# New durations in the table by which a kernel orders its own work

## The chip, the cores and the metric

The kernel runs on one core of one Trainium2 chip. The metric is the device time of one launch in microseconds. The core has a matrix engine (TensorE, PE in the rows; its weight loads are PEld), a vector engine (VectorE, DVE), a scalar engine (ScalarE, ACT), GpSimd (POOL) and the DMA queues (started here from SyncE, SP). Each engine works through its own instructions strictly in the order in which the program emitted them; semaphores make one engine wait for another.

## The reference

Six layers in float32 on a sequence of 1024 (from the fourth on 1040, with 16 meta tokens ahead), width 1024:

```python
# first_block
f1 = swiglu(rms_norm(x, g), w_gate, w_up, w_down);  x = x + 0.5 * rms_norm(f1, g2)      # ffn1, 2816 wide
m  = token_mixer(rms_norm(x, g3), ...);             x = x + rms_norm(m, g4)             # mixer
f2 = swiglu(rms_norm(x, g5), ...);                  x = x + 0.5 * rms_norm(f2, g6)      # ffn2
# token_mixer: 8 causal softmax heads with a decay (fox) and 4 pairs of softmax heads whose difference is taken (diff)
# second_block, on concat(meta, x)
h = rglru_ssd_layer(h)         # even layer: a gated linear recurrence and a chunked state-space scan
# odd layer: 16 heads of stick-breaking attention
z        = q @ k.T * 64**-0.5
log_keep = where(before, log_sigmoid(-z), 0);  csum = cumsum(log_keep)
weights  = where(before, exp(log_sigmoid(z) + csum[-1] - csum), 0)
o        = (weights @ v) * silu(g);            h = h + o @ w_out
return rmsnorm(h)[16:]
```

## The kernel before

All products are made as three matmuls on split operands (high part times high part, low times high, high times low; `mm3`, L334 to 338), accumulated in PSUM. Whatever comes out of PSUM is therefore taken twice: ACT casts the high part, DVE subtracts it to leave the low part.

**What sets the order.** The program doesn't list its instructions in a fixed order. Each piece of work is a generator, a thread, that yields pairs of an engine (P for PE, A for ACT, V for DVE, G for POOL, D for a DMA) and an estimated duration, and then emits the instruction. `Sched` (L109 to 197) keeps for each engine the time at which it will be free, and for each thread the time at which its input is there; `run` always takes the thread whose request can start first, ties by the thread's priority and then its age:

```python
            start = max(ready, self.free[eng])
            switch = self.switch(th[3])
            key = (start + self.TABLE * switch, th[0], th[1])
```

`ready` is the end of the thread's last step, plus HOP = 0.45 us when that was on another engine; TABLE = 0.8 us is the price of changing ACT's function table. The estimates come from four functions at L93 to 106: `pe(n, passes)`, `act(n)`, `dve(n, speed)` and `pool_tt(n)`, n being the columns of the operand. A duration in them thus changes no instruction; it changes which of two instructions is emitted first. Priorities: the evacuation of transposed weights and the value products 0, attention scores and weights 1, weight streams 2, evacuations of projections 3, projections themselves 5.

**The odd stage**, on which the prediction dwells. 16 heads in 8 pairs. For each block of 128 queries: PE makes scores `psc` (L1540, 1541, with a mask matmul L1543); `weights` (L2263 to 2281) puts two sigmoids on ACT (`kt`, `pt`), a running product over the row on DVE (`tensor_tensor_scan`, L2275) and the product of both on DVE (L2279). Then `pv_group` (L1558 on): PE transposes the weights into PSUM (`ptr`, L1607); `pt_evac` lets ACT cast the high part (`th`, L224) and DVE the low part (`tl`, L1552); PE multiplies `th` and `tl` with the values into `po` (L1587). Two `th`, three `tl`, three `ptr` banks are in rotation. Between these, PE's filler is the projection of later head pairs (`pq`, `pk`, `pv`, `pg`: L336 to 338 and L1525 to 1527), which waits for nothing but its PSUM banks (two, freed by an ACT and a DVE step each). The mixer does the same with softmax in place of `weights`. **The even stage** has 1024- and 1040-column operations on DVE (L2553, 2781, 3002), the recurrence (L3015) and the gate product `sz` (L2601), which frees the bank of the projection `pe`. The feed-forward stages are streams of large matmuls.

Of the kernel before, what the change touches and what calls it, by code (L numbers as in the profile page):

```python
# [22 lines left out]
L = M + S  # L23
# [71 lines left out]


def act(n):
    return 0.07 + 0.92e-3 * n


def dve(n, speed=1):
    return 0.08 + 1.045e-3 * n / speed


def pool_tt(n):
    return 0.2 + 2.1e-3 * n


class Sched:  # L109
# [91 lines left out]
class Ctx:  # L201
# [53 lines left out]
    def act_t(self, *args, **kw):  # L255

        self.pin = self.after_pin(self.nc.scalar.activation(*args, **kw))
# [171 lines left out]
class Stream:  # L429
# [38 lines left out]
    def split(self, raw, hi, lo, n, ev, eng, free=True):  # L468
        nc = self.c.nc
        yield ("A", act(n))  # L470
        nc.scalar.copy(hi, raw)
        t = yield (eng, pool_tt(n) if eng == "G" else dve(n))
        (nc.gpsimd if eng == "G" else nc.vector).tensor_sub(lo, raw, hi.bitcast(F32))  # L473
        if free:
            self.r_raw.release(t)
        if ev is not None:
            ev.set(t)
# [898 lines left out]
class Attention:  # L1376
# [30 lines left out]
    def event(self, *key):  # L1407
        return self.ev.setdefault(key, Ev())
# [365 lines left out]
def mixer_stage(c, A, rows0, prm, w_in, forget_b, lams, subln, rope, w_out, gpost, res, rows):  # L1774
# [3 lines left out]
    with ExitStack() as ctx:  # L1778
# [11 lines left out]
        def gate(lf, h):  # L1790
            yield T.r_ps["mm"]
            ps = c.ps("mm", "pg")
            t = yield from gemm(c, ps[:8], W.w["gate"], A, HALVES[h], T.ev_A[h])
            sch.spawn(gate_evac(lf, HALVES[h], ps), 1, t)
            return t

        def gate_evac(lf, tok, ps):
            yield r_rx
            x = pp.tile([8, 512], F32, tag="rx", name="gx", bufs=2)
            e = pp.tile([8, 512], F32, tag="ry", name="ge", bufs=2)  # L1800
            t = yield ("V", dve(512))
            nc.vector.tensor_scalar(x, ps[:8], fb, None, op0=ALU.add)
            T.r_ps["mm"].release(t)
            yield ("A", act(512))
            nc.scalar.activation(e, x, AF.Abs)
            yield ("A", act(512))
            nc.scalar.activation(e, e, AF.Exp, scale=-1.0)
            yield ("A", act(512))
            nc.scalar.activation(e, e, AF.Ln, bias=1.0)
            yield ("V", dve(512, 2))  # L1810
            nc.vector.tensor_scalar(x, x, 0.0, None, op0=ALU.min)
            t = yield ("V", dve(512))
            nc.vector.tensor_sub(lf[:, tok], x, e)
            r_rx.release(t)
            if tok is HALVES[1]:
                cum = pm.tile([8, S], F32, tag="bc", name="cum", bufs=2)
                yield ("V", dve(1024))
                nc.vector.tensor_tensor_scan(cum, c.one[:8].to_broadcast([8, S]), lf, 0.0, op0=ALU.mult, op1=ALU.add)
                t = yield ("D", 0.3)
                nc.sync.dma_start(cD, cum)  # L1820
                r_bc.release(t + 1.0)
                r_bc.release(t + 1.0)
                T.event("cum").set(t + 2.0)
# [132 lines left out]
        def softmax(segs, m, pt, cb, ev, r):  # L1956
            ns = len(segs)
            small = lambda nm: c.small.tile([P, 2], F32, tag=nm, name=nm, bufs=8)
            mx, sm = small("mx"), small("sm")
            for s, ps in enumerate(segs):  # L1960
                yield ("V", dve(m))
                if cb is not None:
                    nc.vector.tensor_tensor_reduce(ps[:, :m], ps[:, :m], cb[:, s * m:s * m + m], 1.0, 3e38,
                                                   ALU.add, ALU.min, accum_out=mx[:, s:s + 1])
                else:
                    nc.vector.tensor_reduce(mx[:, s:s + 1], ps[:, :m], axis=AX.X, op=ALU.min)
            if ns == 2:
                yield ("V", 0.2)
                nc.vector.tensor_tensor(mx[:, 0:1], mx[:, 0:1], mx[:, 1:2], op=ALU.min)
            for s, ps in enumerate(segs):  # L1970
                t = yield ("A", act(m))
                nc.scalar.activation(pt[:, s * m:s * m + m], ps[:, :m], AF.Exp, bias=mx[:, 0:1], scale=-1.0,
                                     accum_out=sm[:, s:s + 1])
                T.r_ps["sc"].release(t)
            yield ("V", 0.2 * ns)
            if ns == 2:
                nc.vector.tensor_add(sm[:, 0:1], sm[:, 0:1], sm[:, 1:2])
            nc.vector.reciprocal(sm[:, 0:1], sm[:, 0:1])
            n = ns * m
            if cb is not None:  # L1980
                yield ("V", dve(n, 2))
                nc.vector.tensor_scalar(pt[:, :n], pt[:, :n], sm[:, 0:1], None, op0=ALU.mult)
            r.append(sm[:, 0:1])
            ev.set(sch.time)
# [205 lines left out]
def odd_stage(c, A, rows0, prm, w_in, w_out, res, final, out):  # L2190
# [3 lines left out]
    with ExitStack() as ctx:  # L2194
# [68 lines left out]
        def weights(ps, w, kt, k0, m, before, scanned, done):  # L2263

            yield ("A", act(m))
            nc.scalar.activation(kt[:, k0:k0 + m], ps[:, :m], AF.Sigmoid, scale=-1.0)
            t = yield ("A", act(m))
            nc.scalar.activation(w[:, k0:k0 + m], ps[:, :m], AF.Sigmoid)
            T.r_ps["sc"].release(t)
            if before is not None:  # L2270
                yield before

            t = yield ("V", dve(m))
            rev = kt[:, k0:k0 + m][:, ::-1]
            nc.vector.tensor_tensor_scan(rev, rev, c.one.to_broadcast([P, m]), kt[:, k0 + m:k0 + m + 1],  # L2275
                                         op0=ALU.mult, op1=ALU.mult)
            scanned.set(t)
            t = yield ("V", dve(m))
            nc.vector.tensor_mul(w[:, k0:k0 + m], w[:, k0:k0 + m], kt[:, k0 + 1:k0 + m + 1])  # L2279
            if k0 == 0:  # L2280
                r_kt.release(t)
                done.set(t)
# [187 lines left out]
LH = L // 2  # L2470
# [28 lines left out]
def even_stage(c, A, rows0, prm, w_in, lru_wa, lru_wx, dt_bias, a_log, ssd_d, w_out, meta, res, rows, later):  # L2499
# [151 lines left out]
    def dt_tile(nm):  # L2651
        dts[nm] = yield from SL.get(nm)
        return dts[nm][1][:NH, :L]
# [14 lines left out]
    def dt_rest():  # L2668
        for i in range(4):
            yield event("dt", i)  # L2670
        l = yield from dt_tile("l")
        dt, cut, ac = (dts[nm][1][:NH, :L] for nm in ("dt", "cut", "ac"))
        yield ("A", act(L))
        nc.scalar.activation(l, dt, AF.Abs)
        yield ("A", act(L), SET_LNEXP)
        act_t(l, l, AF.Exp, scale=-1.0)
        yield ("A", act(L), SET_LNEXP)
        act_t(l, l, AF.Ln, bias=1.0)
        yield ("A", 0.2, SET_LNEXP)
        act_t(na, na, AF.Exp)  # L2680
        yield ("V", dve(L))
        nc.vector.scalar_tensor_tensor(dt, dt, 0.0, l, op0=ALU.max, op1=ALU.add)
        yield ("V", 0.2)
        nc.vector.tensor_scalar(na, na, -1.0, None, op0=ALU.mult)

        nc.gpsimd.memset(cut, 1.0)
        for t0, _ in CHUNKS:
            nc.gpsimd.memset(cut[:, t0:t0 + 1], 0.0)
        yield ("V", dve(L, 2))
        nc.vector.tensor_scalar(l, dt, na, None, op0=ALU.mult)  # L2690
        yield ("V", dve(L))
        nc.vector.tensor_tensor_scan(ac, cut, l, 0.0, op0=ALU.mult, op1=ALU.add)
        t = yield ("D", 0.5)
        nc.sync.dma_start(aD, ac)
        event("aD").set(t + 2.0)

        yield ss
        psd = c.ps("ss", "psd")[:, :288].rearrange("p (c a h) -> p c a h", c=9, a=2)
        yield ("P", 1.0)
        for i, (t0, T) in enumerate(CHUNKS):  # L2700
            nc.tensor.transpose(psd[:T, i, 0], dt[:, t0:t0 + T], c.ident[:NH, :NH])
            nc.tensor.transpose(psd[:T, i, 1], ac[:, t0:t0 + T], c.ident[:NH, :NH])
        t = yield ("V", 0.6)
        nc.vector.tensor_copy(dT[:M, 0], psd[:M, 0])
        nc.vector.tensor_copy(dT[:, 1:], psd[:, 1:])
        ss.release(t)
        for i, _ in dts.values():
            SL.release(t + 1.0, i)
        event("dT").set(t)
# [270 lines left out]
    def lru_rest(b, h, r, ig, t_, v):  # L2980
# [28 lines left out]
        t = yield ("V", dve(L))  # L3009
        nc.vector.tensor_mul(vf, vf, gf)  # L3010
        SL.release(t, ii)
        for j in range(2):
            u = 2 * b + j
            t = yield ("V", dve(LH, 0.5))
            nc.vector.tensor_tensor_scan(t_[:, j], r[:, j], v[:, j], 0.0 if h == 0 else carry[:, u:u + 1], op0=ALU.mult,  # L3015
                                         op1=ALU.add)
            if h == 0:
                nc.gpsimd.tensor_copy(carry[:, u:u + 1], t_[:, j, LH - 1:LH])
# [290 lines left out]
```

## Time and profile before

| | |
|---|---|
| time before, median of 3 runs | 3578.08 us (3573.04 to 3578.96) |
| profiled execution, own time | 3577.13 us |
| its span | 3575.4 us, 51885 instructions |
| PE | 3430.7 us busy, 96% |
| DVE | 2749.9 us busy, 77% |
| ACT | 1700.6 us busy, 48% |
| POOL | 326.1 us busy, 9% |
| granted TensorE clock, mean of the span | 0.987 |

The stages follow each other on PE; those named below are the mixer (730 to 1250 us of the span), the even stage (2010 to 2600) and the odd stage (2835 to 3460). Busy times count durations; as two neighbouring instructions of an engine can overlap, starts are what tells how fast it takes the next one.

### The profile page before, as it was taken

What the parts mean: (1) busy time and instruction counts of PE and PEld (TensorE: products, weight loads), DVE (VectorE), ACT (ScalarE), POOL (GpSimd) and SP (SyncE); (2) the same over time, 40 slices, a digit from 0 to 9 for tenths busy, and PEclk for the clock granted to TensorE, in tenths of its full rate; (3) what the DMA queues carried; (4) which work ended last, traced back from release to release, by engine and by line L of the source; (5) the groups of instructions that cost most, each with busy time, mean ns of one, the idle gap of its engine ahead of it and who ended that gap; (6) DMA issues with size and microseconds to landing.
All of it is one profiled execution on the core that took longest, in us unless ns stands there. A gap on an engine that the chain in (4) does not pass through costs nothing.

```text
span 3575.4 us, 51885 instructions
## 1 busy us (share of the span) xinstructions
PE 3430.7 (96%) x19675; PEld 2925.6 (82%) x19675; DVE 2749.9 (77%) x5050; ACT 1700.6 (48%) x3451; POOL 326.1 (9%) x355
## 2 busy tenths in 40 slices
PE   8999999899999999999999899998999999999998
PEld 6788888678888877888888899988878888888877
DVE  8876699988888769666799779578633688878784
ACT  5323245556666643232345447447422465656561
POOL 0111144000000001111351000000000000000000
PEclk9999999999999999999999999999999999999999
DMA  5542372311211551323552334244473110111133
GB/s 183 178 132 89 113 284 83 128 58 44 73 41 36 179 168 60 123 89 109 195 197 72 108 64 86 61 87 90 139 244 95 57 36 28 33 31 31 33 134 107
DMA packets 305842, 366.07 MB, mean 102 GB/s; under 512 B 18644, under 2 KB 221568, under 8 KB 305592
## 3 DMA queue, kind: packets, MB, share of 16 engines
q1 hardware_dynamic: 299800, 341.71, 30.7%
q10 hardware_dynamic: 5792, 21.04, 1.6%
q8 instruction: 155, 2.54, 0.3%
q14 instruction: 95, 0.78, 0.1%
HBM read 267.58 MB, written 95.13 MB: 101 GB/s over the span
## 4 chain that ended last, share of the span: by engine, by line
PE 73%; DVE 17%; ACT 4%; issue 3%; DMA 2%; SPq 0%; POOL 0%; DVEq 0%; ACTq 0%; POOLq 0%
PE pst L337 7%; PE pst L336 7%; PE pst L338 7%; PE po L1587 3%; PE pe L336 3%; PE pe L338 3%; PE pe L337 3%; DVE kt L2275 3%; PE pdn L337 2%; PE pdn L338 2%; PE pdn L336 2%; PE ptr L1607 2%; PE pwo L3100 2%; PE pwo L3101 2%; PE pwo L3102 2%
## 5 line engine op out<-in xcount | busy, mean ns | idle before, releaser
L336 PE MATMUL pe<-Ah,wh 128*128 128x260 f32 (+1 forms) x1184 | 340.6, 288 | 21.9 <-DVE sz L2601 8.2
L338 PE MATMUL pe<-Ah,wl 128*128 128x260 f32 (+1 forms) x1184 | 337.1, 285 | 0.0
L337 PE MATMUL pe<-Al,wh 128*128 128x260 f32 (+1 forms) x1184 | 336.4, 285 | 0.0
L224 ACT CAST wh<-w 128x512 fp32r<-128x512 f32 x280 | 162.1, 619 | 252.7 <-PE pst L337 160.2
L942 DVE TENSOR_TENSOR sg<-sg,pst 128x512 f32<-128x512 f32 x280 | 187.1, 684 | 104.8 <-PE pst L338 104.4
L1006 POOL TENSOR_TENSOR h<-h 128x512 f32<-128x512 f32 x88 | 136.2, 1547 | 1332.9 <-DVE h L988 1327.7
L337 PE MATMUL pst<-Al,wh 128*128 128x512 f32 x640 | 253.7, 396 | 0.0
L336 PE MATMUL pst<-Ah,wh 128*128 128x512 f32 x640 | 252.2, 394 | 0.0
L338 PE MATMUL pst<-Ah,wl 128*128 128x512 f32 x640 | 252.1, 394 | 0.0
L473 DVE TENSOR_TENSOR wl<-w,wh 128x512 fp32r<-128x512 f32 x280 | 212.0, 784 | 50.4 <-ACT wh L224 49.0
L336 PEld LDWEIGHTS pe<-Ah,wh 128*128 128x128 f32 (+1 forms) x1184 | 223.4, 189 | 26.2 <-DVE sz L2601 8.5
L337 PE MATMUL pdn<-dl,dh 128*128 128x512 f32 x592 | 230.8, 390 | 1.9 <-DVE dl L1099 1.9
L224 ACT CAST th<-ptr 128x512 fp32r<-128x512 f32 (+2 forms) x344 | 171.6, 515 | 125.4 <-PE ptr L1607 78.7
L338 PE MATMUL pdn<-dh,dl 128*128 128x512 f32 x592 | 230.3, 389 | 0.0
L1552 DVE TENSOR_TENSOR tl<-ptr,th 128x512 fp32r<-128x512 f32 (+2 forms) x344 | 197.5, 592 | 41.8 <-ACT th L224 38.4
L336 PE MATMUL pdn<-dh 128*128 128x512 f32 x592 | 229.1, 389 | 0.0
L337 PEld LDWEIGHTS pe<-Al,wh 128*128 128x128 f32 (+1 forms) x1184 | 223.0, 189 | 1.0
L338 PEld LDWEIGHTS pe<-Ah,wl 128*128 128x128 f32 (+1 forms) x1184 | 222.8, 188 | 0.8
L2275 DVE TENSOR_TENSOR_SCAN kt<-kt,onec 128x392 f32<-128x392 f32 (+5 forms) x224 | 204.2, 916 | 16.8 <-ACT kt L224 14.9
L224 ACT CAST wh<-wr 128x1024 fp32r<-128x1024 f32 (+2 forms) x116 | 119.0, 1026 | 182.7 <-PE pwo L3101 80.3
L336 PE MATMUL pst<-T,wh 128*128 128x512 f32 x480 | 187.3, 393 | 8.7 <-ACT T L224 8.7
L337 PE MATMUL pst<-T,wh 128*128 128x512 f32 x480 | 188.1, 392 | 0.4 <-DVE T L835 0.4
(550 smaller groups left out, 10023.6 us busy)
## 6 DMA issues: line engine op xcount, KB each, us to landing
hD<-h SPq DMA_DIRECT2D x22, 1792.0 KB, 8.1
w<-in_ffn_w_gate_dram SPq DMA_DIRECT2D x20, 1024.0 KB, 5.4
w<-in_ffn_w_up_dram SPq DMA_DIRECT2D x20, 1024.0 KB, 8.0
d<-hD SPq DMA_DIRECT2D x18, 1024.0 KB, 5.4
wr<-in_even_w_in_dram SPq DMA_DIRECT2D x36, 512.0 KB, 4.3
wo<-prer SPq DMA_DIRECT2D x32, 512.0 KB, 3.6
wr<-in_odd_w_in_dram SPq DMA_DIRECT2D x32, 512.0 KB, 4.3
wr<-in_w_in_dram SPq DMA_DIRECT2D x24, 512.0 KB, 3.9
```

The source lines that it names most:

```text
L224: self.last = _o(*a, **k)
L336: nc.tensor.matmul(ps, wh, xh, start=start, stop=False)
L337: nc.tensor.matmul(ps, wh, xl, start=False, stop=False)
L338: nc.tensor.matmul(ps, wl, xh, start=False, stop=stop)
L473: (nc.gpsimd if eng == "G" else nc.vector).tensor_sub(lo, raw, hi.bitcast(F32))
L942: nc.vector.tensor_add(dst, src, ps)
L1006: nc.gpsimd.tensor_sub(q[:, o], q[:, a], q[:, b_])
L1552: nc.vector.tensor_sub(tl[:rows, :n], ptr[:rows, :n], th[:rows, :n].bitcast(F32))
L1587: nc.tensor.matmul(po[:, 256 - n:256], vs, (th, tl)[w][:rows, o:o + n], start=(x == 0 and y == 0 and 0 in which), stop=(x == last and y == ...
L1607: nc.tensor.transpose(ptr[:rows, o:o + P], pts[i][:, col:col + rows], c.ident)
L2275: nc.vector.tensor_tensor_scan(rev, rev, c.one.to_broadcast([P, m]), kt[:, k0 + m:k0 + m + 1], op0=ALU.mult, op1=ALU.mult)
L3100: nc.tensor.matmul(ps[n], oh, wh[:, sl], start=(first and k == 0), stop=False)
```

## The change

The functions of the table and what is yielded at four scans, at the softmax (an extra 0.14 for a `tensor_tensor_reduce`, 0.19 for the exponential that also sums) and for a small sum change. HOP, TABLE, `pe`, the priorities and the number of buffers stay.

```diff
 def act(n):
-    return 0.07 + 0.92e-3 * n
+    return 0.16 + 0.87e-3 * n

 def dve(n, speed=1):
-    return 0.08 + 1.045e-3 * n / speed
+    return (0.15 if speed == 1 else 0.21) + 1.05e-3 * n / speed

+def scan(n):
+    return 0.22 + 2.08e-3 * n
+ACCUM = 0.19

 def pool_tt(n):
-    return 0.2 + 2.1e-3 * n
+    return 0.2 + 2.6e-3 * n
...
-                yield ("V", dve(1024))               # cumulative sum of the fox gates
+                yield ("V", scan(1024))
...
-                yield ("V", dve(m))                  # softmax, reduction of a row
+                yield ("V", dve(m) + (0.14 if cb is not None else 0))
...
-                t = yield ("A", act(m))              # softmax, exponential with its sum
+                t = yield ("A", act(m) + ACCUM)
...
-            yield ("V", 0.2 * ns)
+            yield ("V", 0.16 * ns)
...
-            t = yield ("V", dve(m))                  # weights(), odd stage, L2275
+            t = yield ("V", scan(m))
...
-        yield ("V", dve(L))                          # decay sum, even stage
+        yield ("V", scan(L))
...
-            t = yield ("V", dve(LH, 0.5))            # recurrence, even stage, L3015
+            t = yield ("V", scan(LH))
```

(The words after # are added here.) Every engine has the same instructions as before, in another order, but for ACT's table loads, of which the program has 58 before and 54 now. Behind the new functions a line of the changed kernel has a number 8 higher: L1587 is L1595, L1552 is L1560.

PE in the odd stage, where the weights of one group of heads end: before, `po` are the value products, `pv` the projection of a later pair.

```order
L1587 MATMUL po<-th,v_25840 128x256
L1587 MATMUL po<-th,v_25840 128x128
L1587 MATMUL po<-tl,v_25840 128x256 x2
L1525 MATMUL pv<-wh,Ah 128x256
L1526 MATMUL pv<-wl,Ah 128x256
L1527 MATMUL pv<-wh,Al 128x256
L1525 MATMUL pv<-wh,Ah 128x256
L1526 MATMUL pv<-wl,Ah 128x256
L1527 MATMUL pv<-wh,Al 128x256
L1587 MATMUL po<-tl,v_25840 128x256
L1587 MATMUL po<-tl,v_25840 128x128
L1540 MATMUL psc<-ks_25441,qs_25673 128x344
```

PE at the same place now; `ptr` are transposes of the next group, `psc` scores.

```order
L1595 MATMUL po<-th,v_25836 128x256
L1595 MATMUL po<-th,v_25836 128x128
L1595 MATMUL po<-tl,v_25836 128x256 x2
L1549 MATMUL psc<-ks_25437,qs_25668 128x344
L1595 MATMUL po<-tl,v_25836 128x256
L1595 MATMUL po<-tl,v_25836 128x128
L1548 MATMUL psc<-ks_25437,qs_25668 128x344
L1549 MATMUL psc<-ks_25437,qs_25668 128x344
L1615 MATMUL ptr<-ident,pt 128x128 x2
L1548 MATMUL psc<-ks_25438,qs_25668 128x456
L1549 MATMUL psc<-ks_25438,qs_25668 128x456
L1551 LDWEIGHTS identb
```

The six projection matmuls that stood between the `tl` products are gone from there, and scores and the next transposes have come forward.

DVE in the odd stage just ahead of that place, where the low parts `tl` for these products are made, before: scans (`kt`) and products (`pt`) of the weights, `oo` an output, `v` an evacuation of projected values.

```order
L2275 SCALAR_TENSOR_TENSOR kt<-kt,onec 128x456
L2319 TENSOR_TENSOR oo<-oo,g_25444 128x256
L2279 TENSOR_TENSOR pt<-pt,kt 128x456
L2275 SCALAR_TENSOR_TENSOR kt<-kt,onec 128x456
L2279 TENSOR_TENSOR pt<-pt,kt 128x456
L1552 TENSOR_TENSOR tl<-ptr,th 128x256
L1505 TENSOR_TENSOR v_25840<-pv,v_25840 128x128
```

DVE there now.

```order
L2283 SCALAR_TENSOR_TENSOR kt<-kt,onec 128x456
L2287 TENSOR_TENSOR pt<-pt,kt 128x456
L2283 SCALAR_TENSOR_TENSOR kt<-kt,onec 128x456
L1513 TENSOR_TENSOR v_25836<-pv,v_25836 128x128
L1560 TENSOR_TENSOR tl<-ptr,th 128x256
L2287 TENSOR_TENSOR pt<-pt,kt 128x456
L1560 TENSOR_TENSOR tl<-ptr,th 128x512 x2
```

The first `tl` has moved ahead of the second product `pt`, and the value evacuation `v` ahead of `tl`; the output `oo` stands before the first scan.

DVE in the even stage ahead of the gate product `sz`, before: `t` is the recurrence, `ea`, `xc` and `xd` the state-space part, `ll` the low part of a convolved row.

```order
L2838 TENSOR_TENSOR ea<-ea,psy 128x512
L3015 SCALAR_TENSOR_TENSOR t<-r,carry,v 128x520
L2845 SCALAR_TENSOR_TENSOR xc_20733<-xc_20733,dcol,ea 128x128
L2845 SCALAR_TENSOR_TENSOR xc_20734<-xc_20734,dcol,ea 128x128
L2845 SCALAR_TENSOR_TENSOR xc_21612<-xc_21612,dcol,ea 128x128
L2845 SCALAR_TENSOR_TENSOR xc_21613<-xc_21613,dcol,ea 128x128
L2759 TENSOR_TENSOR xd<-psx,dT 128x512
L2942 TENSOR_TENSOR ll<-cv_22481,lh 128x520
L2601 TENSOR_TENSOR sz<-sz,pe 128x260 x2
```

DVE there now; `cbm` is a masked product of the state-space part.

```order
L2846 TENSOR_TENSOR ea<-ea,psy 128x512
L2757 TENSOR_TENSOR cbm<-psb,mask_tri 128x128
L2853 SCALAR_TENSOR_TENSOR xc_20702<-xc_20702,dcol,ea 128x128
L2853 SCALAR_TENSOR_TENSOR xc_20703<-xc_20703,dcol,ea 128x128
L2853 SCALAR_TENSOR_TENSOR xc_21608<-xc_21608,dcol,ea 128x128
L2853 SCALAR_TENSOR_TENSOR xc_21609<-xc_21609,dcol,ea 128x128
L3023 SCALAR_TENSOR_TENSOR t<-r,carry,v 128x520
L2767 TENSOR_TENSOR xd<-psx,dT 128x512
L2609 TENSOR_TENSOR sz<-sz,pe 128x260 x2
```

The recurrence now follows the four `xc` and `ll` is gone from there; `xd` still stands ahead of the first `sz`.

## Rows read from the trace of the kernel before

**Rows 1.** Page, part 1: busy us of each engine, share of span, instructions.

```profile
PE 3430.7 (96%) x19675; PEld 2925.6 (82%) x19675; DVE 2749.9 (77%) x5050; ACT 1700.6 (48%) x3451; POOL 326.1 (9%) x355
```

**Rows 2.** Windows: length; PE, PEld, DVE, ACT, POOL busy (count); clock; DMA share; GB/s.

```profile
2834.94:3459.99 625.05, 588.28 (x4001) 520.06 (x4000) 519.47 (x905) 377.93 (x908) 13.02 (x123) 0.99 0.12 37
730.00:1250.00 520.00, 507.96 (x3141) 431.02 (x3140) 436.62 (x1151) 317.72 (x804) 0.00 (x0) 1.00 0.23 73
2010.00:2600.00 590.00, 561.92 (x4530) 529.62 (x4529) 428.08 (x768) 312.64 (x506) 6.18 (x26) 0.98 0.38 87
```

**Rows 3.** Waits of PE, then of its weight loads: total us, times, longest.

```profile
PE po L1587 <- DVE tl L1552: 22.2, 31, 2.8
...
PE pe L336 <- DVE sz L2601: 8.2, 1, 8.2
...
PEld po L1587 <- DVE tl L1552: 35.2, 53, 3.0
...
PEld po L1587 <- ACT th L224: 24.6, 46, 1.8
```

**Rows 4.** PE by time, odd stage, longest wait on tl: start, duration, instruction.

```profile
2856.34 0.82 PE L1607 MATMUL ptr<-ident,pt 128*128 128x128 f32 x6
...
2858.06 0.40 PE L1587 MATMUL po<-th,v 128*128 128x256 f32 x2
2860.50 0.39 PE L1587 MATMUL po<-tl,v 128*128 128x256 f32 x1 [2.04 <-DVE tl L1552]
```

**Rows 5.** DVE by time, the same place.

```profile
2858.09 1.17 DVE L2275 TENSOR_TENSOR_SCAN kt<-kt,onec 128x456 f32<-128x456 f32 x1
2859.36 0.63 DVE L2279 TENSOR_TENSOR pt<-pt,kt 128x456 f32<-128x456 f32 x1
2860.02 0.42 DVE L1552 TENSOR_TENSOR tl<-ptr,th 128x256 fp32r<-128x256 f32 x1
```

**Rows 6.** Windows of the odd stage: five stretches with little projection.

```profile
2853.03:2865.59 12.56, 10.44 (x68) 9.38 (x67) 11.16 (x19) 6.76 (x17) 0.20 (x2) 0.86 0.04 12
2966.70:2974.80 8.10, 8.10 (x72) 7.98 (x71) 6.29 (x13) 5.26 (x16) 0.20 (x2) 1.00 0.00 0
3115.02:3125.25 10.23, 9.10 (x65) 7.91 (x64) 9.91 (x17) 8.59 (x20) 0.20 (x2) 1.00 0.00 0
3293.95:3306.13 12.18, 9.34 (x68) 8.31 (x68) 11.90 (x21) 7.29 (x17) 0.20 (x2) 1.00 0.03 11
3445.80:3459.99 14.19, 11.06 (x57) 9.20 (x56) 13.68 (x22) 8.82 (x21) 0.30 (x3) 0.83 0.74 250
```

**Rows 7.** Windows of the odd stage: three stretches of almost nothing but projection.

```profile
3037.27:3045.41 8.14, 8.14 (x36) 6.58 (x35) 4.62 (x8) 1.84 (x3) 0.10 (x1) 1.00 0.10 32
3206.94:3215.37 8.43, 8.35 (x37) 6.50 (x36) 5.08 (x11) 1.80 (x3) 0.20 (x2) 1.00 0.31 90
3376.91:3385.03 8.12, 8.12 (x37) 6.50 (x36) 6.44 (x11) 1.66 (x4) 0.20 (x2) 1.00 0.11 34
```

**Rows 8.** DVE by time, even stage.

```profile
2430.09 1.22 DVE L2781 TENSOR_TENSOR ab<-ab,cbm 128x1024 f32<-128x1024 f32 x1
2431.23 1.30 DVE L2553 SCALAR_TENSOR_TENSOR cv<-xb,prm,cv 128x1040 f32<-128x1040 f32 x1
...
2436.82 1.30 DVE L3015 TENSOR_TENSOR_SCAN t<-r,carry,v 128x520 f32<-128x520 f32 x1
...
2443.45 0.76 DVE L2601 TENSOR_TENSOR sz<-sz,pe 128x260 f32<-128x260 f32 x2
```

**Rows 9.** DVE by time, odd stage: a scan, its product, the next scan.

```profile
3000.62 0.77 DVE L2275 TENSOR_TENSOR_SCAN kt<-kt,onec 128x264 f32<-128x264 f32 x1 [1.22 <-ACT kt L224]
3001.49 0.43 DVE L2279 TENSOR_TENSOR pt<-pt,kt 128x264 f32<-128x264 f32 x1
3001.84 0.76 DVE L2275 TENSOR_TENSOR_SCAN kt<-kt,onec 128x264 f32<-128x264 f32 x1
```

**Rows 10.** Groups of ACT by line: busy us, mean ns, idle before.

```profile
L243 ACT ACT_TABLE_LOAD x57 | 73.1, 1283 | 1.0
```

## The prediction

> **What bounds the kernel now.** I read the busy times first: PE works for 3430.7 us, DVE for 2749.9 and ACT for 1700.6 [rows 1]. With PE at 96% of the span only two things can move the time: the 144.7 us in which PE stands (3575.4 - 3430.7), and clock that it loses. The change leaves every engine the same instructions, so it acts through PE's waits alone.
>
> Second, the windows by stage. In the odd stage PE is idle for 36.77 of 625.05 us (5.9%), in the even stage for 28.08 of 590, in the mixer for 12.04 of 520 [rows 2]. The odd stage is also where DVE is fullest for long: 519.47 of 625.05, 83%.
>
> Third, the waits. The largest on PE is that of the value products for the low part `tl`: 22.2 us in 31 waits; the weight loads wait 35.2 us for `tl` and 24.6 for `th` [rows 3]. The even stage has one wait of 8.2 us for `sz`. The longest `tl` wait, followed by time, shows the mechanism: PE has done six transposes at 2856.34 and two `th` products at 2858.06, and then stands until 2860.50, 2.04 us of it put down to `tl` [rows 4]. DVE was not idle: it ran a scan of 1.17 us from 2858.09, its product of 0.63, and only then `tl` [rows 5]. So `tl` waits in DVE's queue behind weights, and PE has no projection in front of it. What decides is thus how much filler the order puts between a transpose and the product that uses it, and what it puts ahead of `tl` on DVE.
>
> **The change part by part.** No duration of the chip changes; I price orders.
>
> *Does the new table tell the truth?* DVE's 1024-column product takes 1.22 us, but the next operation starts 1.14 us after it (2430.09 to 2431.23) [rows 8]. The old price is 0.08 + 1.045e-3 x 1024 = 1.150, the spacing; the new one 0.15 + 1.05e-3 x 1024 = 1.225, the duration. For ordinary operations in a row the new table therefore makes DVE about 0.08 us slower per operation than it is. The scans are the opposite case: a scan of 264 columns with its product goes from 3000.62 to 3001.84, 1.22 us [rows 9]; the old prices give 0.356 + 0.356 = 0.71, the new 0.769 + 0.427 = 1.20. In the odd stage the first error is 0.08 for some 490 operations (905 less 209 scans and 208 products), 39 us of imagined load; the corrected one was 0.5 for some 209 pairs, 105 us. Of the even stage's recurrence the spacing is 1.21 (2436.82 to 2438.03) [rows 8]; old 0.08 + 2.09e-3 x 520 = 1.17, new 1.30: here it becomes worse.
>
> The Trainium skill weighs against the change here too: "Perfetto Trace Analysis", section "Optimizing Scalar/DVE Operations", says that DVE's fixed cost in engine time is about half of what a profiled latency contains, as the write's acknowledgement lies beside the next instruction; the trace agrees (1.14 against 1.22). "VectorE: DVE Perf Modes", section "The DRAIN you can't avoid", says that the next operation doesn't start before the pipe is empty; by that durations would be spacings, every new price would be exact, and the result would be the first rival's; the trace stands against it with the same two numbers.
>
> *Odd stage.* A fuller DVE and ACT in the model makes the evacuations of projections (priority 3) lose to attention (0 and 1): attention runs on with less filler, and the filler comes in lumps. The order shows it right behind the wait above: the six projection matmuls between the `tl` products are gone, scores and the next transposes stand there. I cut PE's order in this stage into 69 stretches of 8 us of issued work, with 0.226 us for 512 columns (36 matmuls in 8.14 us [rows 7]) and 0.12 for 256, and counted the share of projection in each. Before: 5 stretches with less than two fifths, 9 with over four fifths, 55 between. Now: 12, 13 and 44.
>
> The prices come from the trace of before. The five poor stretches are 12.56 + 8.10 + 10.23 + 12.18 + 14.19 = 57.26, 11.45 each [rows 6]. Of the nine rich ones three stand, with a mean of 8.23 [rows 7], which I take for all. The other 55 have (625.05 - 57.26 - 74.1) / 55 = 8.98. The new mix: 12 x 11.45 + 13 x 8.23 + 44 x 8.98 = 639.5, that is +14. Two of the poor stretches ran at a lower clock (0.86 and 0.83, that is partly at the 1.2 GHz level, after PE had waited [rows 4, 6]); taking out that part (14% of 12.56 and 17% of 14.19, 4.2 us) on both sides, the poor cost 10.6 and the sum gives +8. I take the middle, **+11**.
>
> *Mixer.* The same cut gives -2 to +3; PE's 12.04 idle us are the most that could be gained. I take 0.
>
> *Even stage.* The big single wait is DVE's: `xd` stands ahead of the two `sz` of 2443.45 [rows 8], and in the new order too, with the recurrence now close before it. It stays; bounds from both sides are its own 8.2 us, away or twice [rows 3]. I take 0.
>
> *Feed-forward stages.* PE's order is the same there but for a few neighbours: 0.
>
> *Table loads.* Four fewer at 1.28 us each (73.1 / 57) [rows 10], 5.1 us of ACT. ACT works 312.64 of 590 us in the even stage [rows 2]; what covers them is its idle half. Bounds 0 and -5; I take 0.
>
> The sum against the profiled execution's own time: 3577.1 + 11 = **3588 us**; that execution lies 1 us under the median of 3578.08, which I neglect.
>
> **The rivals.**
>
> *R1, faster: the right price of the scans removes waits.* At the longest wait the new DVE order puts the first `tl` ahead of the second product, which takes 0.63 us off it; the correction of 105 us is larger than the new error of 39. Against it: elsewhere transposes and their use have come closer. Counted in PE's work between a group's transposes and its first `tl` product, 24 of 224 groups had less than 2.1 us before (a scan, a product and a `tl` are 1.17 + 0.63 + 0.42 = 2.22 [rows 5]), and 64 have now. Price: outside the five poor stretches PE is idle for 36.77 - 9.22 = 27.6 us (9.22 being their length less their PE time [rows 6]); half of that gone is -14, 3563 us; three quarters, -21.
>
> *R2, no change.* DVE's work is the same, and what it falls behind in poor stretches it regains in the rich ones, where it is busy for 4.6 to 6.4 of 8.1 to 8.4 us [rows 7]; lumps shift waits without adding any. One poor stretch cost nothing (8.10 us with DVE at 6.29 [rows 6]). 3578 us. Against it: there DVE had free time; in the four others it is busy for 89 to 98%.
>
> *R3, much slower.* The poor stretches now follow each other, and DVE's lag piles up from one to the next, from the point where two in a row leave no rich one between. The price is then that of the dearest: 7 more at 14.19 - 8.98 = 5.2 are +36, 3614 us. The other count says nearly that: 40 more close groups at 22.2 / 31 = 0.72 [rows 3] are +29. Against it: most close groups of now have another thread's scores between.
>
> That the change does nothing to the order is excluded by the orders shown.
>
> **How the numbers follow.** Forecast 0.35, R1 0.32, R2 0.25, R3 0.08. The likeliest has its own range of 3583 to 3597 (the sums +8 and +14 with 3 for the mixer and the tables on either side). The whole range takes in R1's three quarters and R3: 3556 to 3614, which leaves about one in seven outside. Changes under 0.2% (7.2 us) can't be told from none; 0.03 of the forecast falls in there. So slower 0.35 + 0.08 - 0.03 = 0.40, same 0.28, faster 0.32.
>
> **What would show it.** Right: busy times of PE, DVE and ACT within some us of before, the odd stage longer by 8 to 14 us, PE's wait on `tl` (now L1560) above 22.2 us by most of that, mixer and feed-forward stages unchanged to 3 us, the `sz` wait of about 8 us still there. R1: the `tl` wait falls to half and the odd stage is under 615 us. R2: the waits have other places and the same sum. R3: lower clock in several stretches of the odd stage. Wrong in its premise: the difference lies in the even stage or the mixer, or is made of clock alone, or DVE's lag in lumps is covered by scores instead of projections, so that my classes by share of projection don't price the time.

## The result and the profile after

The changed kernel takes 3626.22 us (median of 4 runs, 3624.52 to 3628.68) against 3577.51 of the kernel before: ratio 1.0138, 95% interval 1.0125 to 1.0151, **49 us slower**. The direction is that of the forecast, the size is more than four times its +11, and the time lies above the range.

The page of the profile after, span and busy times (its own time is 3627.29 us):

```profile
span 3625.5 us, 51855 instructions
...
PE 3460.4 (95%) x19675; PEld 2945.1 (81%) x19675; DVE 2745.9 (76%) x5050; ACT 1693.8 (47%) x3447; POOL 329.5 (9%) x355
```

Against [rows 1] DVE and ACT have done the same work (-4 and -7 us). PE, with the same 19675 matmuls, is busy 29.7 us longer, and idle for 165.1 us in place of 144.7. So of 50.1 us of span 20.4 are waiting and 29.7 are longer busy time of the same matmuls. The mean granted clock fell from 0.987 to 0.981; 1.3% of 3575.4 and 1.9% of 3625.5 us are 46.5 and 68.9 us of clock lost, so the clock makes up an estimated 22 of the 29.7 us at most, as part of the loss fell in time in which PE stood. The rest of the busy time was not taken apart; e1 below shows busy time growing by 10.4 us at a mean clock of 0.987, as before. One part of it is seen in the rows of the gap below: the last matmul before a gap counts its whole 0.28 us, where the others count only the 0.12 to the next start.

Where it is, by stage: I took the time at which PE reaches the same amount of issued work in both traces. The windows between such points, after; columns as in [rows 2]; mixer, even stage, odd stage:

```profile
747.17:1359.75 612.58, 591.36 (x3473) 498.11 (x3472) 488.52 (x1287) 349.71 (x858) 0.00 (x0) 0.99 0.27 85
2140.25:2622.54 482.29, 444.58 (x3509) 418.49 (x3507) 342.04 (x631) 256.85 (x416) 8.29 (x17) 0.96 0.38 85
2870.11:3509.44 639.33, 595.45 (x4000) 524.81 (x3998) 515.00 (x900) 374.50 (x904) 12.91 (x122) 0.99 0.12 36
```

The mixer and the even stage of before, between the same points:

```profile
748.95:1352.66 603.71, 586.04 (x3475) 496.31 (x3473) 489.77 (x1285) 349.35 (x855) 0.00 (x0) 0.99 0.27 86
2129.65:2588.44 458.79, 434.22 (x3508) 410.27 (x3507) 341.07 (x623) 260.92 (x419) 5.12 (x18) 0.97 0.39 90
```

The odd stage, shown in [rows 2] with 625.05 us, grew by 14.3 (idle +7.1, busy +7.2), the even stage by 23.5 (idle 24.6 to 37.7, busy +10.4), the mixer by 8.9 (idle +3.5, busy +5.3). The feed-forward stages changed by -2.3 and -0.1, the other joints between stages by some +5.

PE's largest waits after, whole span (total us, times, longest):

```profile
PE po L1595 <- ACT th L232: 21.6, 23, 2.2
PE po L1595 <- DVE tl L1560: 12.7, 21, 1.8
PE psc L1548 <- ACT pt L232: 11.6, 19, 1.6
PE pe L344 <- DVE sz L2609: 11.5, 3, 5.3
PE psy L2814 <- DVE ab L2789: 9.6, 7, 3.0
```

Against [rows 3], the wait on `tl` fell from 22.2 to 12.7 us; that on `th`, ACT's half of the same evacuation, rose from 10.6 to 21.6. `sz` went from 8.2 us in one wait to 11.5 in 3, `ab` from 3.2 to 9.6.

What an even-stage wait costs is seen at the first long one, which is new. PE by time there (start, duration, instruction):

```profile
2177.69 0.28 PE L345 MATMUL pe<-Al,wh 128*128 128x260 f32 x1
2177.81 0.28 PE L346 MATMUL pe<-Ah,wl 128*128 128x260 f32 x1
2183.43 0.59 PE L344 MATMUL pe<-Ah,wh 128*128 128x260 f32 x1 [5.34 <-DVE sz L2609]
2183.81 0.42 PE L345 MATMUL pe<-Al,wh 128*128 128x260 f32 x1
2184.02 0.42 PE L346 MATMUL pe<-Ah,wl 128*128 128x260 f32 x1
```

DVE by time in that gap:

```profile
2178.13 1.29 DVE L3023 TENSOR_TENSOR_SCAN t<-r,carry,v 128x520 f32<-128x520 f32 x1
2179.34 0.66 DVE L2846 TENSOR_TENSOR ea<-ea,psy 128x512 f32<-128x512 f32 x1
...
2180.12 1.13 DVE L2853 SCALAR_TENSOR_TENSOR xc<-xc,dcol,ea 128x128 f32<-128x128 f32 x4
2181.17 1.29 DVE L3023 TENSOR_TENSOR_SCAN t<-r,carry,v 128x520 f32<-128x520 f32 x1
2182.38 0.66 DVE L2767 TENSOR_TENSOR xd<-psx,dT 128x512 f32<-128x512 f32 x1
2182.96 0.75 DVE L2609 TENSOR_TENSOR sz<-sz,pe 128x260 f32<-128x260 f32 x2
```

And the windows of the gap and of the 4 us behind it, with the granted clock as the third number from the end:

```profile
2177.81:2183.43 5.62, 0.28 (x4) 0.07 (x2) 5.62 (x12) 3.50 (x8) 0.00 (x0) 0.88 0.89 150
2183.43:2187.50 4.07, 4.07 (x19) 4.07 (x20) 4.03 (x12) 1.31 (x2) 0.00 (x0) 0.50 0.40 54
```

DVE was busy for all 5.62 us: two recurrences, the state-space operations and `xd` stand before the two `sz` that free PE's bank. After the wait the matmuls of 260 columns start every 0.22 us instead of 0.12, at a granted clock of 0.50, which is the 1.2 GHz level, until 2188.8. The wait cost 5.3 us and the 24 matmuls behind it again some 2.4 (0.10 more each).

### The profile page after: what moved, and what is told of

It is laid out like the page before. It is cut to its first block, busy times and chain, and to the rows that moved or that the text cites. A ratio compares the mean times of both kernels' runs of the same rounds, so it can differ in the third digit from the quotient of the medians.

```text
span 3625.5 us, 51855 instructions
## 1 busy us (share of the span) xinstructions
PE 3460.4 (95%) x19675; PEld 2945.1 (81%) x19675; DVE 2745.9 (76%) x5050; ACT 1693.8 (47%) x3447; POOL 329.5 (9%) x355
## 4 chain that ended last, share of the span: by engine, by line
PE 71%; DVE 16%; ACT 6%; issue 3%; DMA 2%; SPq 0%; DVEq 0%; ACTq 0%
PE pst L345 7%; PE pst L346 7%; PE pst L344 7%; PE po L1595 3%; PE pdn L345 3%; PE pdn L346 3%; DVE kt L2283 3%; PE pdn L344 3%; PE pe L344 2%; PE pe L345 2%; PE pe L346 2%; PE ptr L1615 2%; PE pwo L3108 2%; PE pwo L3109 2%; PE pwo L3110 2%
## 5 line engine op out<-in xcount | busy, mean ns | idle before, releaser
L344 PE MATMUL pe<-Ah,wh 128*128 128x260 f32 (+1 forms) x1184 | 343.1, 290 | 21.1 <-DVE sz L2609 11.5
L1560 DVE TENSOR_TENSOR tl<-ptr,th 128x512 fp32r<-128x512 f32 (+2 forms) x344 | 195.8, 590 | 46.6 <-ACT th L232 43.9
```

Source lines behind the costliest of these rows:

```text
L344: nc.tensor.matmul(ps, wh, xh, start=start, stop=False)
L1560: nc.vector.tensor_sub(tl[:rows, :n], ptr[:rows, :n], th[:rows, :n].bitcast(F32))
```

## The experiments

Eighteen kernels ran. The table gives the median, the ratio to the kernel before on the same chip with its interval, and what the mixer, the even and the odd stage gained or lost against before in the profiled execution, at the same points of PE's work. A stage's figure is one execution's; in e5, whose odd stage was ordered by the old prices, the odd stage came out at +0.2. The three stages are not the whole kernel: e14 has another 7.6 us in the joint ahead of the even stage, e19 and e22 have 4.6 and 4.7 there.

| kernel | median us | ratio | mixer | even | odd |
|---|---|---|---|---|---|
| after | 3626.22 | 1.0138 (1.0125 to 1.0151) | +8.9 | +23.5 | +14.3 |
| e1 scans alone | 3590.36 | 1.0032 (1.0019 to 1.0044) | -2.4 | +4.3 | +5.3 |
| e2 act and dve formulas | 3610.68 | 1.0087 (1.0072 to 1.0102) | +4.2 | +18.7 | +5.8 |
| e13 dve formula alone | 3604.97 | 1.0077 (1.0056 to 1.0097) | -0.6 | +19.6 | +8.2 |
| e14 act formula alone | 3613.03 | 1.0099 (1.0079 to 1.0119) | +0.4 | +15.8 | +8.6 |
| e10 after, dve +5 ns | 3617.33 | 1.0106 (1.0086 to 1.0127) | +3.6 | +17.5 | +16.0 |
| e15 after, HOP 0.37 | 3626.46 | 1.0134 (1.0117 to 1.0151) | +5.5 | +29.2 | +15.9 |
| e22 after, evacuations first | 3629.07 | 1.0146 (1.0131 to 1.0161) | +4.4 | +24.0 | +13.2 |
| e5 new table in the even stage | 3602.45 | 1.0061 (1.0044 to 1.0078) | -0.9 | +24.0 | +0.2 |
| e4 before, dve +5 ns | 3600.29 | 1.0061 (1.0046 to 1.0076) | +4.5 | +14.3 | +4.5 |
| e9 before, dve -5 ns | 3577.12 | 0.9999 (0.9988 to 1.0009) | +2.4 | -3.3 | +1.1 |
| e12 before, act +5 ns | 3569.87 | 0.9972 (0.9962 to 0.9983) | -2.4 | -5.7 | -2.6 |
| e20 before, act -5 ns | 3580.54 | 1.0011 (1.0000 to 1.0022) | -0.6 | +3.7 | -3.9 |
| e19 half the new fixed parts | 3591.85 | 1.0042 (1.0023 to 1.0062) | -0.3 | +6.3 | +4.0 |
| e17 both the other way | 3594.14 | 1.0045 (1.0026 to 1.0065) | +1.6 | +4.9 | +8.7 |
| e18 dve the other way | 3602.81 | 1.0071 (1.0048 to 1.0094) | -1.5 | +8.3 | +16.0 |
| e3 after, fixed parts of before | 3594.84 | 1.0044 (1.0029 to 1.0059) | -2.9 | +10.0 | +4.4 |
| e21 after, prices by starts | 3585.94 | 1.0026 (1.0015 to 1.0038) | -1.5 | +3.2 | +10.0 |
| e16 best table of each stage | 3569.16 | 0.9974 (0.9964 to 0.9984) | -0.8 | -4.2 | -2.5 |

**e1_scan**: the kernel after with all prices of before but the scans'.

```diff
 def act(n):
-    return 0.16 + 0.87e-3 * n
+    return 0.07 + 0.92e-3 * n
...
 def dve(n, speed=1):
...
-    return (0.15 if speed == 1 else 0.21) + 1.05e-3 * n / speed
+    return 0.08 + 1.045e-3 * n / speed
...
-ACCUM = 0.19
+ACCUM = 0.0
...
```

> The kernel before with only the four scan places at the new price (act, dve, pool and the softmax terms at the old ones). Three theories of the +49 us. T1, latency counted twice (the new fixed parts contain the end of an operation, which lies beside the next one and which HOP charges already): the scans are innocent, 3565 to 3585 us. T2, the scan price does it (longer recurrences and weights push the evacuations back): 3610 to 3630 us. T3, sensitivity (any small shift of the table moves the greedy order to another one, and before was a tuned point): anywhere from 3585 to 3625 us.

+12 us: too much for T1, far too little for T2, inside T3's wide range. PE's wait on `tl` went the way that my first rival said, from 22.2 to 14.2 us, though not to half:

```profile
PE po L1595 <- DVE tl L1560: 14.2, 19, 2.1
```

but the time was lost elsewhere: PE stands for 147.4 us in all (144.7 before) and is busy 10.4 us longer, 3441.1.

**e2_fixed**: the kernel before with only these two.

```diff
-    return 0.07 + 0.92e-3 * n
+    return 0.16 + 0.87e-3 * n
...
-    return 0.08 + 1.045e-3 * n / speed
+    return (0.15 if speed == 1 else 0.21) + 1.05e-3 * n / speed
```

> The kernel before with only the act and dve formulas at the new values, scans still priced as dve. T1: carries nearly all of the loss, 3610 to 3630 us. T2: 3570 to 3590 us. T3: 3585 to 3625 us, not additive with the scan run (the two differences don't sum to +49 within 15 us).

+32 us, at the lower edge of T1 and inside T3's range: the two formulas carry two thirds of the loss. T3's second condition failed, as 12 and 32 us sum to within 15 of the 49.

**e3_spacing**: after, with

```diff
-    return 0.16 + 0.87e-3 * n
+    return 0.07 + 0.87e-3 * n
...
-    return (0.15 if speed == 1 else 0.21) + 1.05e-3 * n / speed
+    return (0.07 if speed == 1 else 0.13) + 1.05e-3 * n / speed
...
-    return 0.22 + 2.08e-3 * n
+    return 0.14 + 2.08e-3 * n
```

> The kernel after with its fixed parts cut by the 0.08 to 0.09 us by which neighbouring operations overlap in the trace (act 0.07, dve 0.07 and 0.13, scan 0.14), slopes and the other terms as after. T1: the loss goes, 3565 to 3590 us. T2: it stays, 3610 to 3630 us. T3: 3585 to 3625 us.

Two thirds of the loss went. The time is 5 us above T1's range and inside T3's.

**e4_jitter**: before, `0.08` of `dve` as `0.085`.

> Control: the kernel before with the fixed part of dve at 0.085 in place of 0.080, 5 ns that no measurement of an operation here resolves, nothing else. T1 and T2: within 8 us of before, 3570 to 3586 us. T3: a change of more than 10 us either way, most likely slower, 3590 to 3620 us.

+22 us from 5 ns, which T1 and T2 had excluded. T3 was right here, and each other single run has to be read against it.

**e5_even**: after, with a flag set per stage in the top function, so that the new functions return their new value in the even stage alone.

```diff
+NEW = set(['even'])
+STAGE = ['']
...
+def new():
+    return STAGE[0] in NEW
...
 def act(n):
+    if not new():
+        return 0.07 + 0.92e-3 * n
     return 0.16 + 0.87e-3 * n
...
+    STAGE[0] = 'even'
     A4 = even_stage(c, A3, rows3, prm, even_w_in_2[0], lru_w_a_2[0], lru_w_x_2[0], ssd_dt_bias_2,
...
```

> The new table in the even stage alone, the old one in all others. Both theories that are left, S (sensitivity: a near-tie anywhere in the greedy order decides, and before holds a lucky order) and F (the fixed parts count an operation's end twice and so do harm by themselves), expect the stage's own +23 us and nothing elsewhere, as the stages are emitted one after the other: 3597 to 3606 us. If the loss of one stage is handed on to the next or caught up later, the time lies outside, with the odd stage moved by over 3 us.

As both theories said: the even stage holds its +24 by itself, and hands nothing on.

**e9_before_m5** (`dve` 0.075), **e12_before_act** (`act` 0.075), **e10_after_p5** (`dve` 0.155 and 0.215), one number changed in each.

> The kernel before with dve's fixed part at 0.075 in place of 0.080, the mirror image of the +5 ns run. S: slower by 10 to 30 us, 3588 to 3608 us, the even stage +8 to +20. F: a smaller fixed part can't cost anything, 3565 to 3582 us.

> The kernel before with act's fixed part at 0.075 in place of 0.070. S: slower by 10 to 30 us, 3588 to 3608 us. F: within 8 us of before, 3570 to 3586 us.

> The kernel after with dve's fixed parts at 0.155 and 0.215, 5 ns more. S: a draw from the same lot as the shifted kernels before, 3590 to 3615 us, thus faster than after by 10 to 35. F: like after or a little slower, 3620 to 3640 us.

The mirror image costs nothing, act's 5 ns make the kernel 9 us faster, after with 5 ns more is at +39 in place of after's +49. S as I put it (before is a lucky order, every neighbour worse) fell. F held for the mirror image, missed the act run by 0.1 us, and has no place for e4; in e10 the time lies between the two ranges. A spread of some 30 us between neighbours of before stays (-9 to +22), and in these runs it doesn't reach from one table to the other.

**e13_dve_fixed** and **e14_act_fixed**: before with one of e2's two lines.

> The kernel before with the new dve formula alone (0.15 or 0.21 fixed), act and scans as before. The act and dve formulas together cost +32 us. F-dve (the loss comes from DVE, the fuller of the two engines, held to be 0.07 us slower per operation): 3600 to 3615 us, even stage +12 to +20. F-act: 3570 to 3585 us. If both halves are needed: 3585 to 3600 us.

> The kernel before with the new act formula alone (0.16 fixed, slope 0.87e-3). F-dve: 3568 to 3585 us. F-act: 3600 to 3615 us. Both halves needed: 3585 to 3600 us.

Each alone costs about as much as both (28, 36, 32 us); none of the three expectations allows for that. The even stage's waits are different ones, in e13

```profile
PE pe L336 <- DVE sz L2601: 12.8, 3, 6.3
...
PE psy L2806 <- DVE ab L2781: 5.1, 5, 3.1
```

and in e14

```profile
PE psy L2806 <- DVE ab L2781: 18.9, 6, 9.4
...
PE pe L336 <- DVE sz L2601: 1.9, 1, 1.9
```

so the two formulas don't add a cost each; either of them led to an order with more waits.

**e15_after_hop**: after, `HOP = 0.37`.

> The kernel after with HOP at 0.37 in place of 0.45: the 0.08 us by which the new durations reach past the start of the next operation is taken out of the hand-over, so that chains across engines are as long as in the old table and only the engines stay fuller. If the length of chains is what is counted twice: most of the loss goes, 3580 to 3600 us. If the fullness of the engines does it: it stays, 3608 to 3632 us.

Nothing came back. By this run it isn't the length of chains across engines that is counted too high.

**e16_by_stage**: the flag of e5, new table in the first feed-forward stage, `act` 0.075 in the mixer, even and odd stage.

> Stages put together from what each did best: the new table in the first feed-forward stage (-2.3 and -3.1 us in the two kernels with it), act at 0.075 in the mixer, the even and the odd stage (-2.4, -5.7, -2.6 there), the old table in the second feed-forward stage. As the stages' changes add up (the even stage alone gave +24.0 with 0.2 in the odd stage): -13 us, 3562 to 3569 us, faster than before and than the act run of 3570. If a stage's order hangs on what was emitted before it: 3570 to 3585 us.

Faster than before by 8 us, between the two expectations, but no faster than e12 alone: the first stage kept its -2.0, the mixer and the even stage fell short by 1.6 and 1.5 us of what they had in e12. This and e12 are the two kernels that beat both.

**e17_mirror**, **e18_mirror_dve**, **e19_half**, **e20_before_act_m5**: before with other fixed parts.

```diff
-    return 0.07 + 0.92e-3 * n
+    return 0.0 + 0.92e-3 * n       # e17; e18 as before; e19: 0.115; e20: 0.065 (the words after # are added here)
...
-    return 0.08 + 1.045e-3 * n / speed
+    return 0.01 + 1.045e-3 * n / speed      # e17 and e18; e19: 0.115; e20 as before
```

> The kernel before with both fixed parts moved the other way by as much as the new ones were moved: dve 0.01 in place of 0.08, act 0.00 in place of 0.07; slopes and scans as before. One-sided (too large a fixed part overstates the engines): 3563 to 3587 us, even stage -8 to +8. Two-sided (distance from the old table costs): 3595 to 3615 us, even stage +12 to +30.

> The kernel before with dve's fixed part alone at 0.01, the mirror image of the run with dve's new formula (+28 us, even stage +19.6). One-sided: 3563 to 3587 us, even stage -8 to +8. Two-sided: 3595 to 3612 us, even stage +12 to +25.

> The kernel before with both fixed parts half way to the new ones (dve 0.115, act 0.115). If the loss grows with the fixed part: 3585 to 3600 us, even stage +6 to +12. If it is a step that any larger change takes: 3600 to 3615 us, even stage +14 to +25. If only small changes are lucky or unlucky: anything from 3570 to 3600 us.

> One more control: the kernel before with act's fixed part at 0.065 in place of 0.070. From the three shifts of 5 ns so far (+22, -1, -9 us) alone: 3565 to 3602 us, even stage -6 to +15; under 3565 or over 3605 the spread of small shifts has been read too narrow.

The totals don't decide: e17 lies between the two answers, e18 in the two-sided one. By stages, the even stage loses 5 and 8 us when the prices are shifted down, where the whole shift up costs 16 to 29 and half of it (e19) 6. That leans to the one-sided answer, with a loss that grows with the fixed part; it is no more than a lean, as 8.3 lies just past the one-sided range and shifts of 5 ns alone moved this stage by -5.7 to +14.3. In the odd stage down costs 9 and 16, up 6 to 16: two-sided. e20 lies within its range.

**e21_starts**: after, with prices fitted to the starts of neighbours.

```diff
-    return 0.16 + 0.87e-3 * n
+    return 0.08 + 0.85e-3 * n
...
-    return (0.15 if speed == 1 else 0.21) + 1.05e-3 * n / speed
+    return 0.135 + 0.98e-3 * n / speed
...
-    return 0.22 + 2.08e-3 * n
+    return 0.13 + 2.08e-3 * n
```

> The kernel after with prices fitted to starts of neighbouring operations in the traces: dve 0.135 + 0.98e-3 n / speed (128 columns every 0.26 us, 1024 every 1.14), act 0.08 + 0.85e-3 n (512 every 0.53, 1024 every 0.95), scan 0.13 + 2.08e-3 n (520 every 1.21); the rest as after. If truth of the numbers is what counts: 3565 to 3585 us, even stage under +6 and odd under +4. If the rest of the kernel was set around the old table: 3590 to 3615 us.

40 of the 49 us are gone. The even stage is where truth of the numbers would have it, +3.2, its window:

```profile
2127.87:2589.90 462.03, 436.63 (x3509) 412.03 (x3508) 340.02 (x631) 260.75 (x419) 5.34 (x17) 0.97 0.39 88
```

The odd stage is not, +10.0, and the time is 0.9 us past the range, so neither answer holds for the whole kernel. The profiled execution was the slowest of seven, 4.9 us above their median; the stages may be too high by that much in all.

**e22_evac_first**: after, in `half` of the even stage,

```diff
-            sch.spawn(evac(ps, tok, i, bank), 3, t)
+            sch.spawn(evac(ps, tok, i, bank), 0, t)
```

> The kernel after with the evacuations of the even stage's projections at priority 0 in place of 3 (one line, the spawn behind each projection). If the waits on sz come from ties lost to the state-space threads: PE's waits on sz fall from 14 us to under 5, the even stage by 8 to 15 us, 3610 to 3619 us. If DVE's queue only hands the wait to another product (ab): waits on ab grow by about as much, 3620 to 3635 us.

The wait on `sz` (13.9 us in that stage) is no longer among its waits of 0.4 us and more; that on `ab` grew from 9.6 to 29.2, while the `psx` wait beside it stayed:

```profile
PE psy L2814 <- DVE ab L2789: 29.2, 7, 9.5
PE psx L2755 <- ACT xc L232: 6.9, 1, 6.9
```

and the time is about the same, as the second answer said. The wait was only handed from one product of DVE's queue to another.

## Why the prediction was right and wrong

**PE's waits as the only lever: half of the price was missing.** I wrote that waits and lost clock can move the time, then took half of the clock's part out of the odd stage's sum and had no term for it in the others. I also expected PE's busy time within some us of before, and it grew by 29.7 of the 50 us; the lower clock is at most some 22 of them (an estimate, above).

**Odd stage, +11: near in its sum, wrong in its wait.** The classes held: after has 12 poor stretches of 11.53 us (11.45 in the prediction), 13 rich of 8.22 (8.23), 44 between of 8.96 (8.98), together +14.3; the sum without the clock's part, +8, was the wrong correction. Three of the twelve, as in [rows 6]:

```profile
2889.52:2900.87 11.35, 9.42 (x66) 7.87 (x65) 10.91 (x19) 7.87 (x19) 0.20 (x2) 1.00 0.04 13
2991.83:3006.59 14.76, 11.01 (x72) 9.86 (x70) 12.09 (x22) 6.42 (x15) 0.20 (x2) 0.88 0.03 11
3498.20:3509.44 11.24, 9.40 (x61) 7.26 (x58) 10.96 (x20) 9.10 (x22) 0.29 (x3) 1.00 0.88 298
```

But I named `tl` as the wait that would rise. In this stage it fell, and others rose, that on `th` above all; before,

```profile
PE po L1587 <- DVE tl L1552: 21.3, 28, 2.8
PE po L1587 <- ACT th L224: 8.1, 10, 1.3
```

and now

```profile
PE po L1595 <- ACT th L232: 18.8, 18, 2.2
PE po L1595 <- DVE tl L1560: 9.2, 14, 1.8
PE ptr L1615 <- DVE pt L2287: 4.6, 4, 3.5
PE psc L1548 <- ACT pt L232: 4.5, 8, 0.9
```

And the count alone is not a price: e1 has the same 12, 13 and 44, at 11.03 a poor stretch, and lost 5.3 us. That the sum came near is in part luck.

**Even stage, 0: this is the step that failed.** It measured +23.5. I looked at one place, the `sz` wait of 8.2 us, saw it stand in the new order, and bounded the stage by that wait, away or twice. At that place I was right: its waits on `sz` are 8.6 us now. But nothing bounds the stage so: the stage has 3500 matmuls and DVE works for 341 of its 459 us. PE's waits for `sz` and `ab` there were, before,

```profile
PE pe L336 <- DVE sz L2601: 8.2, 1, 8.2
...
PE psy L2806 <- DVE ab L2781: 3.2, 2, 2.5
```

and are now

```profile
PE pe L344 <- DVE sz L2609: 11.5, 3, 5.3
PE psy L2814 <- DVE ab L2789: 9.6, 7, 3.0
...
PE pga L344 <- DVE sz L2609: 2.4, 1, 2.4
```

that is 11.4 us of waits turned into 23.5; the stage's idle time grew by 13.1 and its busy time by 10.4. Two stretches of it, at the same points of PE's work, hold 16 of the 23.5 us; before,

```profile
2129.65:2186.32 56.67, 54.95 (x462) 52.20 (x461) 54.03 (x102) 43.65 (x70) 0.57 (x4) 1.00 0.49 89
2470.10:2533.51 63.41, 58.07 (x477) 54.21 (x476) 51.59 (x91) 44.55 (x70) 0.41 (x2) 0.97 0.36 94
```

and now

```profile
2140.25:2204.63 64.38, 58.16 (x463) 54.95 (x461) 54.47 (x114) 43.13 (x70) 2.17 (x3) 0.95 0.46 74
2494.70:2566.31 71.61, 60.99 (x477) 56.81 (x475) 53.73 (x94) 48.32 (x75) 1.16 (x2) 0.93 0.34 82
```

The first has the new `sz` wait of 5.3 us, the second the waits on `ab`, 3.2 us before and 9.0 now. I had cut the odd stage's order into stretches and not this one's. My own sign of a wrong premise, a difference that lies in the even stage or the mixer, came true.

**Mixer, 0: failed too**, +8.9 us against at most +3. PE's waits for ACT's `pt` there rose from 3.2 to 6.3 us, those for `tl` from 0.7 to 3.0. Other tables gave -2.9 to +5.5, so chance of the order may hold a part; no run took the mixer apart.

**Feed-forward stages and table loads, 0: held** as far as can be seen (-2.3, -0.1; ACT has 4 table loads fewer, and nothing that was gained by it shows). The joints, for which the sum had no term, took some 5 us.

**Is the new table wrong?** I had that from [rows 8]: for operations in a row it charges durations, and starts are closer. Shown: eight kernels with the full new fixed part of dve, act or both in the even stage (after, e2, e5, e10, e13, e14, e15, e22) have an even stage of +15.8 to +29.2; ten with other prices there have -5.7 to +14.3; prices by starts give +3.2. "Perfetto Trace Analysis" of the Trainium skill, section "Optimizing Scalar/DVE Operations", says that a profiled latency holds a part which lies beside the next instruction; e21 is the kernel that takes it out, and 40 of 49 us came back. In the prediction I held the trace's 1.14 against 1.22 us to stand against "VectorE: DVE Perf Modes" of the Trainium skill, section "The DRAIN you can't avoid"; the same paragraph says that a next operation which isn't held starts earlier, so the trace doesn't contradict it.

Not shown is that e21 gained because its prices are true: for most operations they are also close to the old ones (an operation of 512 columns on DVE is 0.64 us, 0.62 in the old table and 0.69 in the new), so nearness to the old table, beside which the rest may have been set, is a rival that no run separates. e3 is nearer still on DVE and has +10.0 in the even stage, but that difference is less than 5 ns have made.

What I had weighed against the error, scans at last at their price, was real in the trace (e1's `tl`) and worth nothing in time.

**Open**: by which choice of the greedy order a larger fixed part leads to the even stage's waits (e15 speaks against the length of chains, e22 against ties lost to the state-space threads); and why the odd stage loses by a shift to either side. That priorities and buffers were set beside the old table would explain the latter; no run tested it.

**The range** ended at 3614, my dearest case of the odd stage alone. It should have had the same kind of end for the even stage and the mixer.

## What to carry to other kernels

A greedy order has a spread of its own: before one believes a change of a few tenths of a per cent in such a table, change one price by a few nanoseconds and see what that does (here -9, -1, +3 and +22 us). A price for an engine's queue is better taken from the distance between starts than from the duration: here the first lost 9 us and the second 49. And where an order changes everywhere, count every stage that has a full engine beside PE; here one wait that stayed in its place said nothing on the rest of its stage.

## What was not expected of the hardware

One wait of PE cost more than its length: behind 5.3 us of standing still the next 24 matmuls of 260 columns started 0.22 us apart rather than 0.12, at a granted clock of 0.50; over the whole kernel 20.4 us more of idle PE came with 29.7 us more of busy PE for the same matmuls, of which the lower clock is an estimated 22 at most.
